# A layer with three kinds of heads on one core: small fp32 products become float32r with their parts stacked in the rows, and the scheduler gets other durations for narrow products

## The chip, the cores and the metric

One Trainium2 chip, one of its eight cores. The kernel is one program; its engines work side by side, each through its own list of instructions in order: TensorE (PE in the profile; PEld is its weight load), VectorE (DVE), ScalarE (ACT), GpSimd (POOL), and SyncE (SP), which here issues the large transfers. The metric is device microseconds of one execution: the median of a few runs. Beside it stands one execution that the profiler recorded.

## The reference

One decoder layer for 512 positions of width 1024, in fp32. Cut to what matters here:

```python
h = rmsnorm(x, norm1_w)
aq, ak, av, bq, bk, bv, br, ba, cq, ck, cv = split(h @ w_in)
# A (6 heads, dilated windows) and C (6 heads, blocks): softmax(q k^T / 8 + bias[bucket(distance)]) v
# B (4 heads, gated linear attention):
log_a = log_sigmoid(ba @ w_a2 + b_a) / 16          # ba: (512, 16), w_a2: (16, 128)
S_t = diag(exp(log_a_t)) S_{t-1} + k_t^T v_t ;  o_t = q_t S_t
y_b = rmsnorm_per_head(o) * gla_norm_w * silu(br)
x = x + concat(y_a, y_b, y_c) @ w_out
x = x + relu(rmsnorm(x) @ w_ff1)^2 @ w_ff2          # 1024 -> 4096 -> 1024
out = rmsnorm(x) * final_norm_w
```

The bias depends on the distance alone, so the kernel makes a table of 12 heads by 640 distances once; where a distance is masked, the table holds a huge number.

## The kernel before

**Numbers.** The large products are made of float32r halves: `hi` is the value rounded by an ACT copy to float32r, `lo` is the rest, made by a DVE subtraction; a product is `hi*hi + lo*hi + hi*lo`, three matmuls into one PSUM bank. The small products were left in plain fp32: the bias table (`vt`: `rb`, 34 rows, times `oneh`), the gate (`zps`: `wa2`, 16 rows, times `alT`), the row scale (`rps`: `ones` times `diag`, which spreads 1/rms of every position over all partitions), the attention transposes (`ptp`), the products of the gated heads (`lp`, `dps`, `ktp`, `op`, `up`) and probabilities times values (`po`).

**Stages on PE.** `first`: columns of the gated heads and of v (`av`, `bq`, `bk`). `v_proj(0)` (`vps`: 4 row tiles t, 24 matmuls each), `qk_proj` for the head pairs p = 0 to 2 (`qkps`: a q and a k bank per pair, 24 matmuls each), `v_proj(1)`, the pairs 3 to 5, `out_proj` (`ops`), then the feed-forward: 32 column tiles (`f`) in four chunks, each chunk followed by seven products of a Strassen-like scheme (`f2X`, `f2Y`, `f2Z`, `f2W`). Between these stand, in the same list, the gated heads (`gla`, `levels`, `carry`) and the attention (`attention`, `softmax`, `turned`, `values`).

**What sets the order.** All stages are Python generators; each yields an instruction, a list of them, a wait for an event, or a take of a resource (a PSUM bank of the groups mm, s, pt, o, g; a buffer; a weight pair `w`). `Plan.run` keeps a clock for every engine, adds `Op.cost` for every instruction, and always issues the candidate that could start first, ties by `prio` and age. Nothing of this runs on the chip: it fixes, at build time, the order in every engine's list. A wrong cost doesn't change what is computed, only where an instruction stands. `late` makes ACT the preferred engine in places where either may copy (`Any`).

**The gated heads' chain.** `gla` scales 16 columns (`alr`), turns them (`alps`), copies them to `alT`, multiplies by `wa2` (`zps`), and makes `la` and its running sum `b` on ACT and DVE. `levels` makes, for 7 levels of a halving scheme, `e` (differences of `b`), its exponential on ACT, and `kq` (DVE). Two levels at a time go to PE as 32 products `lp` of 32 rows and 64 columns; `lp` needs all four banks of s and pt, and DVE frees them with the masked copies `attn<-lmask,lp` (four a level). `v_out` empties each `vps` bank: a scaled copy `v`, then `sg` and `rg` (inputs of the output gate), then the bank is given back.

**Lines.** Every instruction is issued from one line of the planner, so the profile shows L117 for nearly all; the tile names tell them apart. In the changed kernel the same line is L123.

Of the kernel before, what the change touches and what calls it, by code (L numbers as in the profile page):

```python
# [22 lines left out]
BIG = 1e30  # L23
# [9 lines left out]
class Op:  # L33


    def __init__(self, eng, method, args, kw):
# [13 lines left out]
        if eng == "tensor":  # L50
            f = 4 if inner[-1].dtype == F32 and method == "matmul" else 1
            f = f / 2 if args[0].shape[0] == 64 else f / 4 if inner[-1].shape[0] == 32 else f
# [131 lines left out]
def hybrid_block_kernel(ctx: ExitStack, tc: tile.TileContext, xT_d, x_d, w0_d, wv_d, wqk_d, wo_d, w1_d, w2_d,  # L184
# [44 lines left out]
    lmask = consts.tile([128, len(LEVELS), 64], I32)  # L229
    rb = consts.tile([128, 128], F32)  # L230
    bav = consts.tile([128, 1], F32)
    wa2 = consts.tile([128, 128], F32)
    gw = consts.tile([128, 256], F32)
    ones = consts.tile([128, 128], F32)
    eps = consts.tile([128, 1], F32)
    rstd = consts.tile([128, NT], F32)
    nrstd = consts.tile([128, NT], F32)

    oneh = [slot("oneh", shape=(128, 320)) for _ in range(2)]
    alT = slot("alT", shape=(128, 512))  # L240
    xT = [slot("xT") for _ in range(KT)]
# [158 lines left out]
    def load_small():  # L400
        yield ("wait", ("xh", 1))
        for t, d in ((cst, cst_d), (rb[:34, :12], rb_d), (bav, ba_d), (wa2[:16], wa2_d)):
            yield POOL.dma_start(t, d)
        for i in range(2):
            yield POOL.dma_start(oneh[i][:34], oh_d[:, i * 320:(i + 1) * 320])
        fire("consts")
        spawn(bias_table(oneh), 1)
        yield POOL.dma_start(lmask, lm_d)
        for i in range(3):
            for e in range(2):  # L410
                yield POOL.memset(f32(klz[i][e][64 - 64 * e:128 - 64 * e]), 0.0)
        yield POOL.dma_start(gw, bass.AP(tensor=gw_d.tensor, offset=gw_d.offset, ap=[[0, 128], [1, 256]]))

    def row_scale():
# [3 lines left out]
        rsp = bank("mm", "rsp")  # L418
        yield [PE.matmul(rsp[:, 2 * t:2 * t + 2], ssx[:, t * 128:(t + 1) * 128], ones[:, :2], start=True, stop=True)
               for t in range(NT)]  # L420
# [8 lines left out]
        fire("rstd")  # L429
        diag = slot("diag")  # L430
# [11 lines left out]
        fire("R")  # L442

    def bias_table(oneh):
        yield ("wait", "first")
        for i in range(2):
            yield ("take", "mm")
            vt = bank("mm", "vt")
            yield PE.matmul(vt[:, :320], rb, oneh[i], start=True, stop=True)
            vals = slot("vals", shape=(12, 320))  # L450
            yield DVE.tensor_copy(vals, vt[:12, :320])
            give("mm")
            yield POOL.dma_start(tab[:, i * 320:(i + 1) * 320], vals)
        fire("tab")
# [39 lines left out]
    def gla():  # L494
# [4 lines left out]
        yield ("wait", "consts")  # L499
        alr = small("alr", (128, NT, 16))  # L500
# [6 lines left out]
        alps = bank("g", "alps")  # L507
        yield [PE.transpose(alps[:16, t * 128:(t + 1) * 128], alr[:, t, :], ident) for t in range(NT)]
# [126 lines left out]
    def carry(b, kB, qB):  # L635
# [17 lines left out]
        dg = small("dg", (128, 16))  # L653
        yield DVE.tensor_copy(dg, dps[:, :16])
        give("mm")
# [9 lines left out]
    def attention(e):  # L665
# [3 lines left out]
        for p in range(6):  # L669
# [14 lines left out]
            if ("sps", p) in plan.done:  # L684
                give("big")
                give("big")
                if p == 5:
                    for _ in range(3):
                        give("big")
                        give("w")  # L690
                    fire("scores")
# [75 lines left out]
    def v_out(g, t, acc):  # L767

        v = vS[g, t] = slot("v", shape=(128, 384))
        yield Any(ACT.activation(v, acc[:, :384], AF.Copy, scale=rstd[:, t:t + 1]),  # L770
                  DVE.tensor_scalar(v, acc[:, :384], rstd[:, t:t + 1], None, op0=OP.mult), late=dict(vector=late["copy"]))
        fire(("v", g, t))
        cs = slice(g * 128, g * 128 + 128)
        sg, rg = (x[:, t % 2, cs] for x in gates[t // 2])
        yield DVE.tensor_scalar(sg, acc[:, 384:], nrstd[:, t:t + 1], 80.0, op0=OP.mult, op1=OP.min)
        yield DVE.scalar_tensor_tensor(rg, acc[:, 384:], nrstd[:, t:t + 1], gw[:, cs], op0=OP.mult, op1=OP.mult)
        give("mm")
        if g and t % 2:
            spawn(gate(t // 2), 2)

    def v_proj(g):
# [6 lines left out]
        for t in range(NT):  # L788
# [10 lines left out]
            if t == 0:  # L799
                yield ("wait", "rstd")  # L800
                yield ("wait", "consts")
            spawn(v_out(g, t, acc), 1)

# [41 lines left out]
    def qk_proj(p):  # L845
        for i, out in enumerate((q_out, k_out)):
# [4 lines left out]
            give_w()  # L851
            spawn(out(p, acc), 1)

# [364 lines left out]
    def start():  # L1218
# [4 lines left out]
        plan.clock["scalar"] += 1.3  # L1223
        yield DVE.memset(ones, 1.0)
        yield DVE.memset(eps, EPS)
        for z in (rb, wa2, *oneh, alT):
            yield POOL.memset(z, 0.0)
        yield ("take", "mm")
        warm = bank("mm", "warm")
        for _ in range(WARM):  # L1230
            yield PE.matmul(warm[:, :128], ones, ones, start=True, stop=True)
        give("mm")
# [24 lines left out]
def _constants():  # L1257
    d = 511 - np.arange(640)
    oh = np.zeros((34, 640), np.float32)
    oh[_bucket(d), np.arange(640)] = -1.0  # L1260
    cnt = ((d >= 0) & (d <= 128)).astype(np.int32) + ((d >= 0) & (d % 4 == 0)) + ((d >= 0) & (d % 16 == 0))
    oh[32] = np.where(cnt > 0, -np.log(np.maximum(cnt, 1)), BIG)
    oh[33] = np.where(d >= 0, 0.0, BIG)
    ind = np.zeros((2, 12), np.float32)
    ind[0, :6] = 1.0
    ind[1, 6:] = 1.0
    cst = np.zeros((128, 1028), np.float32)
# [58 lines left out]
```

## Time and profile before

| | us |
|---|---|
| median of 3 runs | 596.07 (595.62 to 596.24) |
| the profiled execution's own time | 596.38 |
| its span, first to last instruction | 594.3 |
| PE busy | 581.6 (98%) |
| DVE busy | 428.2 (72%) |
| ACT busy | 321.4 (54%) |
| POOL busy | 18.2 (3%) |

How to read it: the span is that of one execution and lies 2.1 us under its time. A matmul's busy time holds its way through the array, so several overlap and a busy PE need not be at its peak; the distance from one matmul's end to the next's is what it costs in a row, and the chain of waits (what released what, from the last instruction back) shows these distances. An fp32 matmul has two records in the trace, a float32r matmul one. "Idle before" is an engine's wait, with what ended it.

### The profile page before, as it was taken

How to read it: one execution, taken by the hardware profiler on the slowest of the kernel's cores; microseconds unless marked ns; L12 is line 12 of the kernel's file. 1: busy time of each engine (PE TensorE's matmuls, PEld its weight loads, DVE VectorE, ACT ScalarE, POOL GpSimd, SP SyncE). 2: the span in 40 equal slices, each digit the busy share in tenths (PEclk: the TensorE clock that was granted, in tenths of full speed). 3: DMA queues.
4: the chain of work that ended last, by engine and by line, in shares of the span. 5: the costliest groups of instructions: out<-in, count | busy, mean ns of one | idle time of the engine just before them, and what ended most of it. 6: DMA issues, size and time to landing. Idle time of an engine off the chain costs nothing.

```text
span 594.3 us, 8155 instructions
## 1 busy us (share of the span) xinstructions
PE 581.6 (98%) x3021; PEld 481.1 (81%) x3021; DVE 428.2 (72%) x831; ACT 321.4 (54%) x593; POOL 18.2 (3%) x33
## 2 busy tenths in 40 slices
PE   9999999999999999999999999999999999999994
PEld 8977788878886778899888888888888888888883
DVE  5878976864798763565669964499935699764995
ACT  6643337766587663564466425475244664364544
POOL 6010000000000000000000000000000000000021
PEclk9999999999999999999999999999999999999998
DMA  8820431231423620093103642014631036201003
GB/s 299 338 74 2 142 96 47 80 99 57 140 74 113 221 71 2 1 364 139 64 0 117 239 142 71 1 56 157 215 104 35 2 121 235 69 0 36 1 0 142
DMA packets 20391, 61.91 MB, mean 104 GB/s; under 512 B 2544, under 2 KB 2586, under 8 KB 20352
## 3 DMA queue, kind: packets, MB, share of 16 engines
q1 hardware_dynamic: 19728, 60.37, 29.6%
q0 software_dynamic: 480, 1.02, 0.6%
q8 instruction: 24, 0.39, 0.3%
q14 instruction: 15, 0.12, 0.1%
q10 hardware_dynamic: 144, 0.01, 0.0%
HBM read 59.25 MB, written 2.13 MB: 103 GB/s over the span
## 4 chain that ended last, share of the span: by engine, by line
PE 89%; DVE 8%; ACT 1%; issue 1%; DVEq 0%
PE f L117 30%; PE f2X L117 12%; PE qkps L117 11%; PE ops L117 7%; PE f2Z L117 5%; PE vps L117 5%; PE f2Y L117 4%; PE sps L117 2%; PE po L117 2%; PE ptp L117 2%; PE av L117 2%; DVE x L117 1%; PE bq L117 1%; PE bk L117 1%; DVE attn L117 1%; PE f2W L117 1%
## 5 line engine op out<-in xcount | busy, mean ns | idle before, releaser
L117 PE MATMUL f<-yh,wh 128*128 128x512 f32 (+1 forms) x288 | 105.4, 366 | 0.0
L117 PE MATMUL f<-yl,wh 128*128 128x512 f32 (+1 forms) x288 | 105.3, 365 | 0.0
L117 PE MATMUL f<-yh,wl 128*128 128x512 f32 (+1 forms) x288 | 105.2, 365 | 0.0
L117 DVE TENSOR_TENSOR wl<-wraw,wh 128x1024 fp32r<-128x1024 f32 (+1 forms) x68 | 77.9, 1158 | 34.1 <-ACT wh L117 34.0
L117 ACT ACTIVATE wh<-wraw 128x1024 fp32r<-128x1024 f32 (+1 forms) x67 | 66.4, 1009 | 52.8 <-PE f L117 31.4
L117 DVE TENSOR_TENSOR wl<-w2raw,wh 128x1024 fp32r<-128x1024 f32 x48 | 59.1, 1241 | 47.2 <-ACT wh L117 43.6
L117 ACT ACTIVATE wh<-w2raw 128x1024 fp32r<-128x1024 f32 x48 | 50.3, 1052 | 53.4 <-PE f L117 36.8
L117 PEld LDWEIGHTS f<-yh,wl 128*128 128x128 f32 x288 | 54.3, 189 | 8.8
L117 PEld LDWEIGHTS f<-yl,wh 128*128 128x128 f32 x288 | 54.3, 189 | 8.7
L117 PEld LDWEIGHTS f<-yh,wh 128*128 128x128 f32 x288 | 54.3, 189 | 8.7
L117 PE MATMUL f2X<-wh,Ah 128*128 128x512 f32 x112 | 43.6, 389 | 0.0
L117 PE MATMUL f2X<-wh,Al 128*128 128x512 f32 x112 | 43.6, 389 | 0.0
L117 PE MATMUL f2X<-wl,Ah 128*128 128x512 f32 x112 | 43.6, 389 | 0.0
L117 PE MATMUL qkps<-xh,wh 128*128 128x512 f32 x96 | 40.3, 419 | 0.1
L117 PE MATMUL qkps<-xl,wh 128*128 128x512 f32 x96 | 37.6, 392 | 0.0
L117 PE MATMUL qkps<-xh,wl 128*128 128x512 f32 x96 | 37.6, 391 | 0.0
L117 ACT ACTIVATE P<-P,mn 128x512 f32<-128x512 f32 (+3 forms) x48 | 26.6, 554 | 11.5 <-DVE mn L117 11.3
L117 ACT ACTIVATE h<-f 128x512 f32<-128x512 f32 x32 | 18.7, 583 | 20.8 <-PE f L117 20.8
L117 DVE CUSTOM_DVE_ANT_0 P<-sps,nb 128x512 f32<-128x512 f32 (+3 forms) x48 | 22.3, 480 | 8.8 <-PE sps L117 8.5
L117 PE MATMUL vps<-wh,xh 128*128 128x512 f32 x64 | 27.9, 437 | 0.0
L117 ACT ACTIVATE junk<-x 128x512 f32<-128x512 f32 x16 | 10.1, 630 | 30.4 <-DVE x L117 30.4
L117 ACT ACTIVATE Ah<-s 128x512 fp32r<-128x512 f32 x32 | 18.8, 619 | 13.9 <-DVE s L117 13.9
(223 smaller groups left out, 1210.6 us busy)
## 6 DMA issues: line engine op xcount, KB each, us to landing
wraw<-in_w SPq DMA_DIRECT2D x32, 512.0 KB, 3.4
w2raw<-in_w SPq DMA_DIRECT2D x32, 512.0 KB, 4.1
wraw<-in_wqk SPq DMA_DIRECT2D x12, 512.0 KB, 3.5
wraw<-in_wv SPq DMA_DIRECT2D x8, 512.0 KB, 6.6
wraw<-in_wo SPq DMA_DIRECT2D x8, 512.0 KB, 3.7
nb<-tab SPq DMA_DIRECT2D x12, 256.0 KB, 3.9
wraw<-in_w SPq DMA_DIRECT2D x8, 264.0 KB, 6.8
xT<-in_xT SPq DMA_DIRECT2D x8, 256.0 KB, 6.7
```

The lines of the kernel that those rows point to most:

```text
L117: getattr(getattr(self.nc, op.eng), op.method)(*op.args, **op.kw)
```

## The change

**Numbers.** `rb`, `oneh`, `wa2`, `alT`, `ones` and `diag` become float32r, with the parts of both factors stacked in the rows, so that one matmul sums the parts' products: rows 0 to 31 of `rb` hold the table's rounded values and rows 32 to 63 the rest, against the same one-hot rows twice; the three rows for masks stand at 64. `wa2` holds hi, hi and lo at rows 0, 32 and 64, `alT` holds hi, lo and hi there (the 16 columns are scaled into three groups of 32 and turned together). The row scale alone becomes two matmuls, with `dh` and `dl`. A new stream, `stacked`, rounds the small tables (3 ACT copies, 2 DVE subtractions); `bias_table` and the gate wait for it. `alT` is now copied by ACT, and one DVE subtraction follows.

**Scheduler.** Other costs for PE, two lines of them:

```diff
-            self.cost = 0.002 + (max(n, 250) / 2400 * f if method == "matmul" else 0.054)
+                self.cost = 0.0135 + long
```

(`long` is max(n, 250)/2400; a transpose counts 0.109, an fp32 matmul of 32 rows 0.031, other fp32 matmuls at least 0.212.)

**Moves.** `v_out` copies `v` on ACT always, copies the gate's columns to `rg` on ACT, gives the bank back, and makes `sg` and `rg` on DVE from SBUF with a later priority; `dg` is copied by ACT; of the weight pairs given back after the last attention, two come after pair 4 instead; `v_out`, `q_out` and `k_out` get priority 0.5.

```diff
 def load_small():
-        for t, d in ((cst, cst_d), (rb[:34, :12], rb_d), (bav, ba_d), (wa2[:16], wa2_d)):
+        for t, d in ((cst, cst_d), (rbx[:32], rb_d[:32]), (rb[64:67, :12], rb_d[32:]), (bav, ba_d), (wax[:16], wa2_d)):
...
+        spawn(stacked(), 1)
 def row_scale():
+        yield ACT.activation(dh, diag, AF.Copy)
+        yield DVE.tensor_tensor(dl, diag, f32(dh), op=OP.subtract)
...
-        yield PE.matmul(rps, ones, diag, start=True, stop=True)
+        yield [PE.matmul(rps, ones, d, start=(d is dh), stop=(d is dl)) for d in (dh, dl)]
+    def stacked():
+        yield ACT.activation(rb[:32, :12], rbx[:32], AF.Copy)
+        yield DVE.tensor_tensor(rb[32:64, :12], rbx[:32], f32(rb[:32, :12]), op=OP.subtract)
+        yield ACT.activation(wa2[:16], wax[:16], AF.Copy)
+        yield ACT.activation(wa2[32:48], wax[:16], AF.Copy)
+        yield DVE.tensor_tensor(wa2[64:80], wax[:16], f32(wa2[:16]), op=OP.subtract)
+        fire("stacked")
 def bias_table(oneh):
+        yield ("wait", "stacked")
 def gla():
-            yield DVE.tensor_scalar(alr[:, t, :], acc_v[t][:, 256:272], rstd[:, t:t + 1], None, op0=OP.mult)
+            yield DVE.tensor_scalar(alr[:, t, :, :16], acc_v[t][:, None, 256:272].to_broadcast([128, 3, 16]), rstd[:, t:t + 1],
+                                    None, op0=OP.mult)
...
-        yield DVE.tensor_copy(alT[:16], alps[:16, :])
+        yield ACT.activation(alT[:96], alps[:96], AF.Copy)
+        yield DVE.tensor_tensor(alT[32:64], alps[32:64], f32(alT[32:64]), op=OP.subtract)
         give("g")
+        yield ("wait", "stacked")
 def carry(b, kB, qB):
-        yield DVE.tensor_copy(dg, dps[:, :16])
+        yield ACT.activation(dg, dps[:, :16], AF.Copy)
 def v_out(g, t, acc):
-        yield Any(ACT.activation(v, acc[:, :384], AF.Copy, scale=rstd[:, t:t + 1]),
-                  DVE.tensor_scalar(v, acc[:, :384], rstd[:, t:t + 1], None, op0=OP.mult), late=dict(vector=late["copy"]))
+        yield ACT.activation(v, acc[:, :384], AF.Copy, scale=rstd[:, t:t + 1])
...
-        yield DVE.tensor_scalar(sg, acc[:, 384:], nrstd[:, t:t + 1], 80.0, op0=OP.mult, op1=OP.min)
-        yield DVE.scalar_tensor_tensor(rg, acc[:, 384:], nrstd[:, t:t + 1], gw[:, cs], op0=OP.mult, op1=OP.mult)
+        yield ACT.activation(rg, acc[:, 384:], AF.Copy, scale=nrstd[:, t:t + 1])
         give("mm")
+        yield ("prio", 2)
+        yield DVE.tensor_scalar(sg, rg, 80.0, None, op0=OP.min)
+        yield DVE.tensor_tensor(rg, rg, gw[:, cs], op=OP.mult)
```

The rest of the diff moves the zeroing of these tiles (POOL zeroes `alr` too) and lays out the constants on the host in the new rows.

**What the lists become.** On PE the matmuls stay the same but for one more in `rps`. From the first `f` on, PE's list differs only in where the last `yps` transposes stand; DVE's and ACT's there differ by instructions that change places with a neighbour or two.

First place: DVE from the end of `first` to the gate's `la` (`alr` the 16 gate columns, `vals` the bias table's values, `Rn` the row scale, `wl` a weight's lo half). Before:

```order
L117 TENSOR_SCALAR alr<-av_118,rstd 128x16
L117 COPY vals<-vt 12x320
L117 TENSOR_TENSOR wl<-wraw,wh 128x1024
L117 TENSOR_SCALAR Rn_95<-rps 128x512
L117 COPY alT<-alps 16x512
L117 COPY vals<-vt 12x320
L117 TENSOR_SCALAR la<-zps,bav 128x512
```

Now:

```order
L123 TENSOR_SCALAR alr<-av_121,rstd 128x3x16
L123 COPY vals<-vt 12x320
L123 TENSOR_TENSOR wl<-wraw,wh 128x1024
L123 TENSOR_SCALAR Rn_98<-rps 128x512
L123 COPY vals<-vt 12x320
L123 TENSOR_TENSOR alT<-alps,alT 32x512
L123 TENSOR_SCALAR la<-zps,bav 128x512
```

The copy of `alT` has left DVE, and a subtraction that makes its lo rows stands behind the second `vals`.

Second place: DVE between the first and the second group of `lp` (a level is told by its shape: 4x64 and 8x32 are the first group's, 16x16 and 32x8 the second's). Before:

```order
L117 TENSOR_SCALAR sg<-vps,nrstd 128x128
L117 SCALAR_TENSOR_TENSOR rg<-vps,nrstd,gw 128x128
L117 TENSOR_TENSOR qk<-qB,kB 128x512
L117 TENSOR_TENSOR kq<-kB,e 128x16x16
L117 TENSOR_TENSOR kq<-qB,e 128x16x16
L117 TENSOR_TENSOR e<-b 128x32x8 x2
L117 COPY_PREDICATED attn_540<-lmask,lp 128x4x64
L117 TENSOR_TENSOR kq<-kB,e 128x32x8
L117 TENSOR_TENSOR kq<-qB,e 128x32x8
L117 TENSOR_TENSOR e<-b 128x64x4 x2
L117 COPY_PREDICATED attn_541<-lmask,lp 128x4x64
```

Now:

```order
L123 TENSOR_TENSOR qk<-qB,kB 128x512
L123 TENSOR_TENSOR kq<-kB,e 128x16x16
L123 TENSOR_TENSOR kq<-qB,e 128x16x16
L123 TENSOR_TENSOR e<-b 128x32x8 x2
L123 COPY_PREDICATED attn_572<-lmask,lp 128x4x64
L123 COPY_PREDICATED attn_573<-lmask,lp 128x4x64
L123 COPY_PREDICATED attn_574<-lmask,lp 128x4x64
L123 TENSOR_TENSOR kq<-kB,e 128x32x8
L123 TENSOR_TENSOR kq<-qB,e 128x32x8
L123 TENSOR_TENSOR e<-b 128x64x4 x2
L123 COPY_PREDICATED attn_575<-lmask,lp 128x4x64
```

`sg` and `rg` have left this stretch, and three of the masked copies that free a bank stand together ahead of the next level's `kq`.

Third place: PE from the first group of `lp` to the first weights of the next stage (`dps` and `ktp` are small products of `carry`). Before:

```order
L117 MATMUL lp<-kq 128x64 x32
L117 MATMUL dps<-cst,qk 128x4 x4
...
L117 MATMUL lp<-kq 128x64 x32
L117 MATMUL ktp<-cst,ek 128x128 x3
```

Now:

```order
L123 MATMUL lp<-kq 128x64 x32
...
L123 MATMUL dps<-cst,qk 128x4 x4
...
L123 MATMUL ktp<-cst,ek 128x128 x3
...
L123 MATMUL lp<-kq 128x64 x32
```

Left out are `vps` matmuls. Between `first` and the first group of `lp` they are 51 before and 60 now; between the first and the second group 21 before and 27 now; between the second and the third 18 before, and now 9 with 15 `qkps`; ahead of the last group 6 with 9 `qkps` before, and 18 `qkps` now. Up to the first `op` (a product of the gated heads) all 96 `vps` are done in both lists; of `qkps` there are 21 before and 54 now.

## Rows read from the trace of the kernel before

**Rows 1.** The page's chain that ended last, shares of the span by engine

```profile
PE 89%; DVE 8%; ACT 1%; issue 1%; DVEq 0%
```

**Rows 2.** Chain in order of time (start us, us, what): feed-forward and end

```profile
346.05 43.52 PE f L117 x192
...
558.21 4.77 PE f2Y L117 x21
...
579.85 0.61 DVE x L117
```

**Rows 3.** The same chain, from the end of first to the gate

```profile
30.23 0.54 PE vt L117 x2
...
31.46 1.00 PE rps L117 x2
...
33.16 0.44 PE alps L117 x4
...
33.92 0.78 PE vt L117 x2
...
35.39 0.87 PE zps L117 x2
```

**Rows 4.** The same chain, gated heads

```profile
55.73 1.96 PE lp L117 x58
57.70 0.81 PE ktp L117 x3
58.50 5.40 PE vps L117 x18
63.90 1.98 PE lp L117 x64
...
70.25 1.07 PE lp L117 x26
...
74.72 0.84 PE op L117 x8
```

**Rows 5.** Timeline of PE (start us, us, instructions, [idle before]), 53 to 70 us

```profile
53.45 0.39 PE L117 MATMUL vps<-wl,xh 128*128 128x512 f32 x1
54.07 1.06 PE L117 MATMUL lp<-kq 32*128 32x64 f32 x6 [0.23 <-DVE attn L117]
55.73 1.96 PE L117 MATMUL lp<-kq 32*128 32x64 f32 x58 [0.60 <-DVE dg L117]
...
69.40 0.44 PE L117 MATMUL lp<-kq 32*128 32x64 f32 x6
```

**Rows 6.** Windows: A:B us, PE, PEld, DVE, ACT, POOL busy, PEclk, DMA, GB/s

```profile
57.70:61.10 3.40, 3.40 (x10) 2.81 (x11) 3.40 (x11) 2.50 (x4) 0.00 (x0) 0.50 0.00 0
61.10:74.70 13.60, 13.20 (x139) 10.71 (x139) 12.81 (x23) 3.83 (x5) 0.00 (x0) 1.00 0.47 155
...
257.00:563.00 306.00, 306.00 (x1445) 257.52 (x1444) 219.25 (x308) 153.21 (x234) 0.00 (x0) 1.00 0.29 101
563.00:580.00 17.00, 16.97 (x75) 13.71 (x73) 16.99 (x29) 7.99 (x16) 5.27 (x4) 1.00 0.00 0
```

**Rows 7.** Timeline of DVE, 52 to 54 us: one level of the gated heads

```profile
52.49 0.42 DVE L117 TENSOR_TENSOR kq<-qB,e 128x256 f32<-128x256 f32 x1
52.82 0.75 DVE L117 TENSOR_TENSOR e<-b 128x256 f32<-128x256 f32 x2
53.49 1.09 DVE L117 COPY_PREDICATED attn<-lmask,lp 128x256 f32<-128x256 int32 x3
54.49 0.42 DVE L117 TENSOR_TENSOR kq<-kB,e 128x256 f32<-128x256 f32 x1
```

**Rows 8.** Timeline of ACT: a weight's hi half in first, the row scale's copy

```profile
18.54 0.63 ACT L117 ACTIVATE wh<-wraw 128x528 fp32r<-128x528 f32 x1
...
32.50 0.60 ACT L117 ACTIVATE R<-rps 128x512 f32<-128x512 f32 x1 [1.24 <-PE rps L117]
```

**Rows 9.** What PE waited for: us in total, times, longest us

```profile
PE sps L117 <- DVE mn L117: 0.5, 1, 0.5
```

More of the change, by code (lines that the diff above doesn't have):

```diff
@@ L50, in __init__ @@
         if eng == "tensor":
-            f = 4 if inner[-1].dtype == F32 and method == "matmul" else 1
-            f = f / 2 if args[0].shape[0] == 64 else f / 4 if inner[-1].shape[0] == 32 else f
-            self.cost = 0.002 + (max(n, 250) / 2400 * f if method == "matmul" else 0.054)
+            wide, long = inner[-1].dtype == F32, max(n, 250) / 2400
+            if method != "matmul":
+                self.cost = 0.109
+            elif wide and inner[-1].shape[0] == 32:
+                self.cost = 0.031
+            elif wide:
+                self.cost = 0.002 + max(n / 600 / (1 + (args[0].shape[0] == 64)), 0.21)
+            else:
+                self.cost = 0.0135 + long
         elif eng == "scalar":
@@ L237, in hybrid_block_kernel @@
     nrstd = consts.tile([128, NT], F32)
-    oneh = [slot("oneh", shape=(128, 320)) for _ in range(2)]
-    alT = slot("alT", shape=(128, 512))
+    oneh = [slot("oneh", F32R, (128, 320)) for _ in range(2)]
+    alT = slot("alT", F32R)
+    alr = slot("alr", shape=(128, NT, 3, 32))
     xT = [slot("xT") for _ in range(KT)]
@@ L418, in row_scale @@
         rsp = bank("mm", "rsp")
-        yield [PE.matmul(rsp[:, 2 * t:2 * t + 2], ssx[:, t * 128:(t + 1) * 128], ones[:, :2], start=True, stop=True)
+        yield [PE.matmul(rsp[:, 2 * t:2 * t + 2], ssx[:, t * 128:(t + 1) * 128], f32(ones[:, :2]), start=True, stop=True)
                for t in range(NT)]
@@ L507, in gla @@
         alps = bank("g", "alps")
-        yield [PE.transpose(alps[:16, t * 128:(t + 1) * 128], alr[:, t, :], ident) for t in range(NT)]
-        yield DVE.tensor_copy(alT[:16], alps[:16, :])
+        yield [PE.transpose(alps[:96, t * 128:(t + 1) * 128], alr[:, t].rearrange("p a b -> p (a b)"), ident) for t in range(NT)]
+        yield ACT.activation(alT[:96], alps[:96], AF.Copy)
+        yield DVE.tensor_tensor(alT[32:64], alps[32:64], f32(alT[32:64]), op=OP.subtract)
         give("g")
+        yield ("wait", "stacked")
         yield ("take", "o")
@@ L686, in attention @@
                 give("big")
+                if p == 4:
+                    give("w")
+                    give("w")
                 if p == 5:
@@ L851, in qk_proj @@
             give_w()
-            spawn(out(p, acc), 1)
+            spawn(out(p, acc), 0.5)
     gates = []
@@ L1223, in start @@
         plan.clock["scalar"] += 1.3
-        yield DVE.memset(ones, 1.0)
+        yield DVE.memset(f32(ones), 1.0)
         yield DVE.memset(eps, EPS)
-        for z in (rb, wa2, *oneh, alT):
+        for z in (f32(rb), f32(wa2), f32(oneh[0]), f32(oneh[1]), alr, f32(alT)):
             yield POOL.memset(z, 0.0)
@@ L1230, in start @@
         for _ in range(WARM):
-            yield PE.matmul(warm[:, :128], ones, ones, start=True, stop=True)
+            yield PE.matmul(warm[:, :128], f32(ones), f32(ones), start=True, stop=True)
         give("mm")
@@ L1258, in _constants @@
     d = 511 - np.arange(640)
-    oh = np.zeros((34, 640), np.float32)
-    oh[_bucket(d), np.arange(640)] = -1.0
+    oh = np.zeros((67, 640), np.float32)
+    for i in (0, 32):
+        oh[i + _bucket(d), np.arange(640)] = -1.0
     cnt = ((d >= 0) & (d <= 128)).astype(np.int32) + ((d >= 0) & (d % 4 == 0)) + ((d >= 0) & (d % 16 == 0))
[L1262 to L1266, printed above, removed]
+    few = np.where(cnt > 0, -np.log(np.maximum(cnt, 1)), BIG).astype(np.float32)
+    oh[64] = (few.view(np.int32) & ~4095).view(np.float32)
+    oh[65] = np.where(cnt > 0, few - oh[64], 0.0)
+    oh[66] = np.where(d >= 0, 0.0, BIG)
+    ind = np.zeros((3, 12), np.float32)
+    ind[:2, :6] = 1.0
+    ind[2, 6:] = 1.0
     cst = np.zeros((128, 1028), np.float32)
```

17 lines of the change are left out of this document (9 added, 8 removed).

## The prediction

> **What bounds the kernel now.** I read the chain that ended last first: 89% of it is PE [rows 1]. That alone could mean a busy or a waiting PE, so I looked at distances. In the feed-forward 192 matmuls of 512 columns follow each other in 43.52 us [rows 2], 0.227 us each; from 257 to 563 us PE is busy for all 306 us of the window, at a granted clock of 1.00 (2.4 GHz) [rows 6]. So the second half runs at one matmul after the other, and nothing in it can be gained but by removing matmuls. What can change lies ahead of it. There the chain shows fp32 products dearer than their columns [rows 3], two groups of small products at which PE waited [rows 4, 5], and a stretch of 3.4 us at a granted clock of 0.50 (1.2 GHz) [rows 6]. PE is the engine to follow; each of the others matters only where PE waits for it.
>
> Does time gained early arrive at the end? The tail from 563 us is DVE's: it is busy for 16.99 of 17.00 us there [rows 6], but the chain enters it from PE's `f2Y`, which ends at 562.98, and its last add into x starts at 579.85 [rows 2]. Between 257 and 563 us DVE has 87 us idle (306 less 219.25 [rows 6]), so its tail isn't held up by earlier work and starts when PE gets there. I take early gains as passed on whole.
>
> **Part by part. The fp32 products.** A float32r matmul of 512 columns costs 0.227. `zps` takes 0.87 as fp32 and becomes one matmul: 0.64 less. `rps` takes 1.00 and becomes two: 0.55 less. The two `vt` took 0.54 each without their wait [rows 3]; 320 columns of float32r lie between 0.14 (by columns) and 0.227, and I take 0.15, since the columns scale: 0.78 less for both (0.63 at worst). `alps` keeps its four transposes (0.44 [rows 3]); more rows come out, the columns that go in are the same. Sum: **1.97 us** off PE.
>
> **What it adds elsewhere.** `stacked` puts three small ACT copies and two small DVE subtractions into `first`. ACT makes the last weight's hi half of `first` at 18.54 [rows 8] and PE ends `first` only at 30.23 [rows 3]; even at the price of a full 512-wide copy (0.60 [rows 8]) three copies are 1.8 us, against some 8 us of lead that ACT has by then. The price is nothing as long as that lead stands, 1.8 us if it were gone. POOL's queue gets one transfer and one zeroing more ahead of the others; its tables are first needed shortly before `vt` at 30.23, and PE waits for no transfer there before. `dh` and `dl` (one copy of 0.60, one subtraction of 0.61 as the add of [rows 2]) lie behind the six `vps` that now stand ahead of `rps`. The output gate's columns cost ACT eight more copies, at most 0.60 each, and DVE as many instructions as before; ACT is the idler engine.
>
> **The wait before the second `vt`.** PE idled 0.33 and the product took 0.78 for 0.54 [rows 3]: 0.57 lost. It takes the bank that `rps` gives back after a copy on ACT and one on DVE, about 1.3 us behind `rps`. Now six `vps` (1.36) and `alps` (0.44) lie between: covered, **0.57 us** off.
>
> **The gate's chain, followed once.** From 30.23: `vt` 0.15, six `vps` 1.36, `rps` 0.45, six `vps` 1.36, `alps` 0.44, that is 33.99; `vt` 0.15 and six `vps` bring PE to `zps` at 35.50. Its input is ready 0.60 (ACT) and 0.61 (DVE, behind the second `vals`) after `alps`: 35.2 to 35.4. The new subtraction fits by 0.1 to 0.3 us; if it doesn't, PE waits and all of the gate's chain with it, a few tenths. `zps` ends at 35.73 where it ended at 36.26, and 42 `vps` (9.52) later PE is at the first `lp` at 45.25. Before, PE reached it at 45.7 with 9 `vps` less behind it.
>
> **The second group of `lp`.** The `vps` that started at 53.45 was through at 53.68; a group takes 1.98 [rows 4]; it ended at 57.69 [rows 4, 5]. Waits for the masked copies cost 57.69 - 53.68 - 1.98 = 2.03 us. Now: the first group ends at about 47.3, and 27 `vps` (6.12), `dps` (0.9) and `ktp` (0.33) bring PE to the second at 54.6 (a transpose is 0.11 by `alps`, and `dps` has eight records of that size). On DVE one of a level's two `kq` costs 0.33 (52.49 to 52.82), its `e` pair 0.67, three masked copies 1.00 [rows 7]. In the new list stand, between the second level's `kq` (done at 45.3 to 46.0) and the last masked copy of the first group: three `e` pairs ahead of the copies and one among them, three `kq` pairs, eight copies (2.7) and two 512-wide products (1.2), together 8.6: 53.9 to 54.6. PE arrives at that time or just after. **2.0 us** off, at worst 1.2.
>
> **The clock.** At 57.70, after 4.0 us in which PE had nothing but `lp` and waits, the granted clock fell to 0.50 until 61.10 [rows 6]. `ktp` took 0.81 for 0.33 and 18 `vps` 5.40 for 4.08 [rows 4]: 1.80 lost. The third group of `lp`, 1.98 us long with full matmuls on both sides, brought no fall: 1.00 from 61.1 to 74.7 [rows 6]. In the new order every group stands so. I take **1.8 us** off. The Trainium skill, "TensorE: Matmul & The Clock Gate", section "Why this matters for your kernels", warns of idle gaps between bursts of matmuls several times longer than the 0.23 and 0.60 here. By that rule the fall would not come from these waits and would not leave with them, and the sum would be 1.8 us smaller; the fall in this trace speaks against the rule as it stands.
>
> **The last group.** Half a group is 0.99; its first records started at 69.40 [rows 5] and it ended at 71.32 [rows 4], so 0.9 was lost to masked copies. Now 18 `qkps` (4.08) lie between the third group and it: 0.7 off. The waits around `dps` (0.3) go too, since it now stands behind three more `vps`.
>
> **Sum by the first `op`:** 1.97 + 0.57 + 2.0 + 1.8 + 0.7 + 0.3 = 7.3 us. A count confirms it without any of these terms. From 30.23 on, the new list holds up to the first `op`: 96 `vps` and 54 `qkps` (150 x 0.227 = 34.0), `rps`, `zps`, `vt`, `alps` (1.4), three and a half groups of `lp` (some 7.5 with their first matmul), `dps`, `ktp`, `up` (1.7): 44.6, so `op` at 74.9. Before it came at 74.72 [rows 4] with 33 `qkps` less done: 33 x 0.227 - 0.2 = 7.3.
>
> **The attention.** Its order is new throughout, and the trace of before can't show its waits. It had one wait of 0.5 at `sps` [rows 9]; some such waits go, some come. Bounds: 1.0 off (that one and as much again in smaller ones) to 2.0 on (one more like the second `lp`). Following DVE through the first pair I find PE waiting some tenths at `sps`, no more, and I take 0.5 off, nearest to the row. **The feed-forward's** neighbours change places by one weight subtraction (1.1 us) at most, with its inputs ready one product (5.44) ahead: nothing, at worst 0.5, since PE had no wait in those 306 us while DVE had 87 idle.
>
> **The forecast.** 7.3 + 0.5 = 7.8 off the profiled execution's 596.38 is 588.6. The median of the runs is 0.3 under that execution: **588.3**, with 586.0 to 589.4 as its own range.
>
> **Rivals.** (1) The clock falls all the same: small products cause it, not the waits. For it: `lp` and `dps` stand close again, with few `vps` between; against it: the third group kept 1.00 around it [rows 6], and no wait is left that I can find. 590.1. (2) The scheduler's order brings new waits at the attention, two of the size of the second `lp`: 592.3. The stretch from 257 us on has no slack that could give them back. (3) The new order gives nothing: what is gained at `lp` is lost at `sps`, and only the passes are left. 596.1 - 2.0 = 594.1, hardly beyond what can be told from no change (about 0.2%, 1.2 us). (4) Slower: the attention of a pair now starts while the gated heads still hold DVE, and PE waits for softmax at every one of the six pairs. At 2.0 us each that is 12.2, less the 0.5 above: 588.3 + 12.2 = 600.5; it decides from 1.5 us a pair on, where 9 us are lost. For it: the earlier start, and ACT's extra copies. Against it: 0.5 us was the longest such wait in all six pairs, and `qkps` or `vps` stand between the steps as before.
>
> **How the numbers follow.** Forecast 0.58, better than its range 0.03, (1) 0.15, (2) 0.11, (3) 0.08, (4) 0.05. Range: from 586.0, the attention's and the feed-forward's waits all gone and small ones with them, to 593.0, case (2) with its bounds; (3) and (4) are left out. Faster: all but (4), half of (3) and a little of (2): 0.88; same 0.07; slower 0.05.
>
> **What would show it.** Right: `zps` a single record of some 0.23 us in the chain; the first `op` near 74.9 with no wait over 0.3 at any `lp`; PEclk at 1.00 from 57 to 62 us; `f` starting some 7.8 earlier; the stretch from there to the end as long as before. Wrong: a window at 0.50 in the gated heads or the attention; PE waiting for `mn`, `th` or a masked copy by more than 1 us in sum; a longer tail.

## The result and the profile after

The changed kernel takes **592.89 us** (median of 6 runs, 592.38 to 593.49); the runs of the kernel before that stood beside it have a median of 596.15. The ratio is 0.9932, with a 95% interval of 0.9913 to 0.9951. So it is faster by 3.3 us, inside the range by 0.1 us, but by less than half of the 7.8 us that the sum promised. The profiled execution took 592.38 us with a span of 590.6, 3.7 less than before.

First the chain that ended last, as the page gives it for the changed kernel, by engine; it answers to [rows 1]:

```profile
PE 83%; DVE 12%; ACT 2%; issue 1%
```

PE's share fell from 89 to 83%, and DVE's rose from 8 to 12%: the path now leaves PE more often. Where it does is seen in the chain in order of time (start us, us, what), here from the end of `first` to the first softmax step, then two rows of the second half. It answers to [rows 2 to 4]:

```profile
29.14 0.15 PE vt L123
...
30.68 0.47 PE rps L123 x2
...
32.97 0.15 PE vt L123
...
34.49 0.44 PE zps L123
...
44.49 1.94 PE lp L123 x64
46.44 0.89 PE vps L123 x3
...
54.03 1.94 PE lp L123 x64
...
61.64 1.98 PE lp L123 x64
63.62 2.30 DVE attn L123 x6
...
80.15 0.68 DVE P L123
80.85 0.04 issue
80.89 1.23 PE sps L123 x4
...
341.13 43.52 PE f L123 x192
```

Up to 63.6 us the chain stays on PE, and no wait stands at any `lp`. One short wait hides inside a row: `zps` takes 0.44 us where 0.23 were expected. A matmul's weights are loaded ahead of it by PEld (for the `vps` before `zps` at 33.88, the matmul itself starting at 34.10), and the load for `zps` waited for DVE's subtraction into `alT`:

```profile
34.43 0.19 PEld L123 LDWEIGHTS zps<-alT,wa 128*128 128x128 f32 x1 [0.37 <-DVE alT L123]
```

Where this load doesn't wait (e3, e7 and e13 below), `zps` takes 0.23. From 63.6 us on, for 17 us, the chain runs through DVE (masked copies, weight subtractions, the q and k of the first pairs, small steps of the gated heads) until `sps` waits for it at 80.89, by 0.37 us. PE isn't idle up to there, it works on `qkps`. The feed-forward is the same to the hundredth of a microsecond, 43.52 us for 192 matmuls, and starts 4.92 us earlier than in [rows 2].

The windows of the changed kernel (A:B us, then busy time of PE, PEld, DVE, ACT and POOL, PEclk, DMA share, GB/s) that answer to [rows 6]:

```profile
57.70:61.10 3.40, 3.40 (x17) 2.82 (x16) 3.37 (x11) 1.79 (x3) 0.00 (x0) 1.00 0.60 179
61.10:74.70 13.60, 13.60 (x142) 11.12 (x141) 11.56 (x20) 3.27 (x4) 0.00 (x0) 1.00 0.23 78
```

The window at 0.50 is gone and PE is busy throughout. What PE waited for (us in total, times, longest) answers to [rows 5, 9]:

```profile
PE sps L123 <- DVE mn L123: 1.2, 3, 0.6
...
PE f2Z L123 <- DVE x L123: 0.9, 1, 0.9
PE yps L123 <- DVE yl L123: 0.6, 1, 0.6
PE ptp L123 <- ACT th L123: 0.3, 1, 0.3
```

The waits at `lp` have left the list. Before, they were these:

```profile
PE lp L117 <- DVE attn L117: 0.6, 2, 0.4
...
PE lp L117 <- DVE dg L117: 0.6, 1, 0.6
```

In their place stand waits at softmax, 1.2 at `sps` where it was 0.5, and a new one at `yps`.

**Where the gain went.** Three points of the two traces can be laid side by side. At the first `vt` the changed kernel is 1.09 us ahead (29.14 to 30.23): this can't be put down to the change, since five of the traces below whose lists are the same up to there (the changed kernel, e4, e6, e11, e12) have that `vt` at 29.1 to 30.1. At the first `op`, at 74.70 where it was 74.72, it has done 33 more `qkps`, 7.5 us of work; less the 1.09 that makes **6.4 us** won between 30 and 75 us. At the first `f` the lead is 4.92, less 1.09: **3.8 us**. So 2.6 us were given back between 75 and 252 us. The list of waits shows about half of it: from there on the waits at `sps`, `ptp` and `yps` come to 2.3 us, and to 1.0 before. After that the list costs 0.3 us more up to PE's end (the longer wait of `f2Z` for x), and the end behind PE 9.0 us where it was 8.0.

### The profile page after: what moved, and what is told of

Read it like the earlier page. It is cut to its first block, busy times and chain, and to the rows that moved or that the text cites. A ratio compares the mean times of both kernels' runs of the same rounds, so it can differ in the third digit from the quotient of the medians.

```text
span 590.6 us, 8146 instructions
## 1 busy us (share of the span) xinstructions
PE 577.4 (98%) x3018; PEld 476.0 (81%) x3018; DVE 426.2 (72%) x830; ACT 327.2 (55%) x610; POOL 18.6 (3%) x35
## 4 chain that ended last, share of the span: by engine, by line
PE 83%; DVE 12%; ACT 2%; issue 1%
PE f L123 30%; PE f2X L123 11%; PE ops L123 7%; PE vps L123 7%; PE qkps L123 6%; PE f2Z L123 6%; PE f2Y L123 3%; DVE wl L123 2%; PE po L123 2%; PE ptp L123 2%; PE av L123 2%; PE sps L123 2%; DVE x L123 2%; DVE P L123 1%; DVE Al L123 1%
## 5 line engine op out<-in xcount | busy, mean ns | idle before, releaser
L123 PE MATMUL ops<-wh,mh 128*128 128x512 f32 x64 | 26.0, 407 | 0.0
L123 PE MATMUL f2Z<-wh,Ah 128*128 128x512 f32 x64 | 25.0, 390 | 0.9 <-DVE x L123 0.9
```

The lines of the kernel that those rows point to most:

```text
L123: getattr(getattr(self.nc, op.eng), op.method)(*op.args, **op.kw)
```

## The experiments

The change has three parts that can be made apart: the **products** in float32r with stacked parts, the **moves** (copies of the output gate and `dg` to ACT, an earlier `give`, priorities of 0.5), and the scheduler's new **durations** for PE. The first four runs take them apart, later ones split the durations by time and by kind. The time from the first `vt` to the first `f` is read from each profile, and leaves out the start and the feed-forward. Ratios are to the runs of the kernel before on the same chip.

| kernel | products | moves | durations | median us | ratio, 95% interval | `vt` to `f` us |
|---|---|---|---|---|---|---|
| before | fp32 | no | old | 596.1 to 596.5 | | 226.6 |
| e2_new_costs | fp32 | no | new | 595.86 | 0.9986 [0.9973, 0.9999] | 225.8 |
| e3_f32r_only | float32r | no | old | 600.74 | 1.0068 [1.0043, 1.0094] | 231.0 |
| e5_moves_only | fp32 | yes | old | 598.17 | 1.0025 [1.0005, 1.0046] | 229.1 |
| e1_old_costs | float32r | yes | old | 592.63 | 0.9926 [0.9899, 0.9952] | 225.0 |
| e14_no_f32r | fp32 | yes | new | 594.10 | 0.9952 [0.9934, 0.9970] | 224.2 |
| e10_v_out_before | float32r | all but the gate's | new | 593.57 | 0.9954 [0.9937, 0.9972] | none |
| changed kernel | float32r | yes | new | 592.89 | 0.9932 [0.9913, 0.9951] | 222.8 |
| e4_lp62 | float32r | yes | new, `lp` 0.062 | 592.66 | 0.9930 [0.9912, 0.9948] | 224.0 |
| e7_old_then_new | float32r | yes | old to 72 us, then new | 596.23 | 0.9987 [0.9964, 1.0009] | 225.1 |
| e6_new_then_old | float32r | yes | new to 72 us, then old | 588.53 | 0.9858 [0.9821, 0.9896] | 219.5 |
| e11_late_dense_old | float32r | yes | from 72 us: dense old | 590.73 | 0.9895 [0.9875, 0.9915] | 221.7 |
| e12_late_rest_old | float32r | yes | from 72 us: all else old | 592.12 | 0.9920 [0.9902, 0.9937] | 222.7 |
| e13_dense_old | float32r | yes | new, dense old | 590.84 | 0.9901 [0.9883, 0.9919] | 222.0 |

**Old durations under the rest of the change (e1).** Its edit:

```diff
-            wide, long = inner[-1].dtype == F32, max(n, 250) / 2400
-            if method != "matmul":
-                self.cost = 0.109
...
-                self.cost = 0.0135 + long
+            f = 4 if inner[-1].dtype == F32 and method == "matmul" else 1
+            f = f / 2 if args[0].shape[0] == 64 else f / 4 if inner[-1].shape[0] == 32 else f
+            self.cost = 0.002 + (max(n, 250) / 2400 * f if method == "matmul" else 0.054)
```

> The changed kernel with the scheduler's durations for PE of before; the float32r products and all moves stay. Theory A (the new durations gain some 4.7 us up to the first `op`, the passes only 1.7, and 2.6 is given back later at softmax, by the new order): 18 `vps` stand between the first two `lp` groups, as few as before (21), so PE waits 1.5 to 2.5 us at the second group and a window at a granted clock of 0.50 follows it; by the first `op` the lead on the kernel before is 2 to 3 us, and it ends at 593 to 595. Rival B (the order brought nothing, the passes all of it): as the changed kernel, 592.5 to 593.5, with no wait at `lp`. Rival C (the copies moved to ACT cause the waits at softmax): waits at `sps` and `ptp` in the attention stay near 4 us.

Measured: 592.63, the same as the changed kernel. It lies 0.4 us below theory A's range, and in rival B's. But it isn't rival B: the waits at `lp` are there. The rows are PE's timeline (with the idle time before each; two more waits of 0.17 stand between these), then a window, as above:

```profile
66.77 0.40 PE L117 MATMUL lp<-kq 32*128 32x64 f32 x2 [0.62 <-DVE attn L117]
...
68.47 1.89 PE L117 MATMUL lp<-kq 32*128 32x64 f32 x26 [0.17 <-DVE attn L117]
```

```profile
68.52:75.35 6.83, 6.83 (x38) 5.66 (x39) 3.29 (x6) 0.00 (x0) 0.00 (x0) 0.50 0.00 0
```

They stand at the last group, not at the second, and in this run a fall of the granted clock to 0.50 over 6.83 us followed, which costs half of it. Not every run has it: three of its six runs have a mean granted clock of 0.997 to 0.998 and take 590.5 to 591.5, three have 0.990 to 0.992 and take 593.8 to 594.7. That is 3 us, as 6.83 us at half speed make it (3.4). In its runs at 0.997 or more this kernel beats the changed one by 2 us: its list loses at `lp`, and from the first `op` to the first `f` it takes 1.6 us less than the kernel before for the same work (178.49 us with 258 `qkps`, against 182.12 with 267). Rival C falls with it: the copies on ACT are in it, and PE has no wait at `sps`.

**Durations alone (e2)** is the same edit the other way round, made in the kernel before.

> The kernel before with the scheduler's new durations for PE alone; no product is float32r and nothing is moved to ACT. 30 `vps` and `dps` stand between the first two `lp` groups. Theory A: no wait over 0.3 us at `lp`, granted clock 1.00 all the way from 10 to 580 us, lead at the first `op` 4 to 5 us, then 1 to 3 given back at `sps` and `ptp`: 592.5 to 594.5. Rival B: the lead at the first `op` is under 1 and the time 595.5 to 596.5. Rival C: the waits in the attention stay as short as before (2.4 us over the pure products), and the time is 591.5.

Measured: 595.86, no better than rival B's bound, though the granted clock was 1.00 all the way. The first part of A holds (no long wait at `lp`), but a wait came up that A hadn't in it, at a `vps` for DVE's `rg`:

```profile
PE vps L123 <- DVE rg L123: 1.4, 1, 1.4
```

So the lead at the first `op` is 2.3 us and not 4 to 5 (42 `qkps` done where it was 21, 2.5 us later from the first `vt`), and 1.4 of it are given back up to the first `f`, within A's 1 to 3.

**float32r alone (e3)** leaves durations, `v_out`, `dg`, the gives and the priorities as before.

> The kernel before with the products in float32r and the stacked parts alone; durations, priorities and the output gate's copies as before. Theory A: 18 `vps` and `dps` between the first two `lp` groups, PE waits 2 us or more at the second, the granted clock falls to 0.50 after it; gain 1.7 (passes) and 0.6 (second `vt`), 593.5 to 595. Rival B: the whole gain of the changed kernel, 592.5 to 593.5. Rival D (the clock's fall in the run of before was chance): the wait is there, but the granted clock stays at 1.00, and it ends 1.8 earlier than A says, 592 to 593.

Measured: 600.74, 4.5 us *slower* than before; no theory had that. The timeline of DVE, and the row of PE that waited for it:

```profile
53.97 0.35 DVE L117 TENSOR_SCALAR sg<-vps,nrstd 128x128 f32<-128x128 f32 x1 [0.48 <-ACT v L117]
...
54.57 0.42 DVE L117 TENSOR_TENSOR kq<-qB,e 128x256 f32<-128x256 f32 x1
54.91 0.34 DVE L117 SCALAR_TENSOR_TENSOR rg<-vps,nrstd,gw 128x128 f32<-128x128 f32 x1
...
55.40 0.47 PE L117 MATMUL vps<-wh,xh 128*128 128x512 f32 x1 [4.37 <-DVE rg L117]
```

`vps` needs a bank, and `v_out` gives one back only after `rg`, which stands in DVE's list behind products and masked copies of the gated heads. PE stood still for 4.37 us, as the first of these windows shows; the others are two falls of the granted clock behind it:

```profile
51.00:55.40 4.40, 0.03 (x2) 0.04 (x1) 3.92 (x13) 2.18 (x4) 0.00 (x0) 1.00 0.00 0
55.75:59.17 3.42, 3.42 (x30) 2.49 (x32) 1.37 (x3) 0.00 (x0) 0.00 (x0) 0.50 0.09 19
72.82:79.65 6.83, 6.83 (x35) 5.57 (x32) 3.80 (x7) 0.00 (x0) 0.00 (x0) 0.50 0.00 0
```

The two falls take 5.1 us of work, the wait 4.4, against some 2 won by the passes; the kernel before has a fall of its own (1.8 us of work) and its waits at `lp` (2.0). Set against each other these make 3.7 us, where 4.5 were measured.

**The moves alone (e5).** The kernel before with, among others:

```diff
-        yield DVE.tensor_copy(dg, dps[:, :16])
+        yield ACT.activation(dg, dps[:, :16], AF.Copy)
...
-        yield DVE.tensor_scalar(sg, acc[:, 384:], nrstd[:, t:t + 1], 80.0, op0=OP.mult, op1=OP.min)
+        yield ACT.activation(rg, acc[:, 384:], AF.Copy, scale=nrstd[:, t:t + 1])
         give("mm")
```

> The kernel before with the moves alone (the output gate's copies and `dg` on ACT, the earlier `give`, the priorities of 0.5); products in fp32, durations of before. Theory A, mended: the moves only take away a wait that the kernel before doesn't have, so the waits at `lp` (2 us at the second group) and the window at 0.50 stay: 595 to 596.5. Rival E (the moves carry most of the gain by themselves): the gated heads are 2 to 4 us shorter and it ends at 592 to 594.

Measured: 598.17, slower than both theories. Here it is the other move that PE waits for. The timeline of ACT, PE's row, and two windows:

```profile
51.50 0.63 ACT L117 ACTIVATE e<-e 128x512 f32<-128x512 f32 x1 [1.50 <-DVE e L117]
52.04 0.17 ACT L117 ACTIVATE dg<-dps 128x16 f32<-128x16 f32 x1
...
52.26 0.90 PE L117 MATMUL ktp<-cst,ek 128*128 128x128 f32 x3 [2.36 <-ACT dg L117]
```

```profile
50.99:57.82 6.83, 5.56 (x15) 4.50 (x16) 5.16 (x16) 1.82 (x4) 0.00 (x0) 0.50 0.00 0
74.89:78.30 3.41, 3.41 (x10) 2.66 (x9) 2.83 (x6) 0.00 (x0) 0.00 (x0) 0.50 0.00 0
```

`dg` frees the bank of `dps`, and stands in ACT's list behind an `e` that itself waits for DVE. In the changed kernel it stands ahead of that `e` (48.15 and 48.23 us in its trace) and nobody waits. The wait is about as long as what the kernel before loses at `lp` (2.0 us by the prediction's working); what makes this kernel slower goes with the clock: nine of its ten runs have a mean granted clock of 0.988 to 0.990 and take 597.4 to 599.3 us, the tenth has 0.994 and takes 595.82. So neither the products nor the moves gain anything alone; what a part is worth depends on the list that it stands in.

**The gate's step of before in the changed kernel (e10).** The step `v_out` alone is put back; the bank of `vps` is again freed by DVE after `rg`.

> The changed kernel, with the output gate's step written as before: the bank of a `vps` product is given back by DVE after `rg`, not by ACT. Theory A, mended by the first four runs (in them PE waited 4.4 us for `rg` where only the products were float32r, 1.4 where only the durations were new, and not at all in the kernels with the moved copies): the bank comes back behind the masked copies on DVE, PE waits 1 to 4 us at `vps` between the first two `lp` groups, and it ends at 594 to 597. Rival: the new order alone keeps PE fed, no wait for `rg` over 0.3 us, 592 to 593.

Measured: 593.57, 0.7 us above the changed kernel, between the two. Its profiled execution took 2057.62 us and can't be laid beside the others, so whether PE waits for `rg` here, and where the 0.7 us lie, stays open.

**The changed kernel without float32r (e14).** The kernel before with the moves of e5 and the durations of e2.

> The changed kernel without its float32r products: the moves and the new durations, with the six products in fp32 as before. By the sum of the passes (1.7 us) and the wait behind the second `vt` (0.6) it takes 2.3 us more than the changed kernel, 595.2. Rival J (what the products gain or lose is the list that they bring about: 21 `vps` between the first two `lp` groups, where PE waits again, up to 2 us and with a fall of the clock): 596 to 598.

Measured: 594.10. The products in float32r (`vt`, `zps`, `rps`) are worth 1.2 us in the final list, about half of what the sum of the passes said (2.3 with the second `vt`). The traces show why: by the first `op` this kernel is 2.4 us behind the changed one, as the sum had it (its lead on the kernel before is 4.0 there, with 36 `qkps` done), and from there to the first `f` it gives back 1.5 us where the changed kernel gives back 2.6. Rival J's waits did not come.

**`lp` with its measured duration (e4).** The edit is one number, 0.062 for 0.031.

> The changed kernel with 0.062 us for each of the narrow `lp` products in the scheduler instead of 0.031 (a group of 32 takes 1.94 to 1.98 us in the trace, which is 0.062 each). Theory A: up to the first `op` the list is the same but for three `vps` or `qkps`, so the lead there is the same within 0.3 us; the attention of the first pairs is mixed otherwise, with the third `up` and its `op` later, and what is given back there changes by up to 1.5 us either way: 591.5 to 594. A rival (the wrong duration of `lp` is what makes the waits at softmax): the waits of the attention fall from 4.2 to 2.4 us and it ends at 591.

Measured: 592.66, as A says; the number itself doesn't make the waits. A's lead at the first `op` did not come in the profiled run: it was 4.2 us, not 6.4, with a fall of the clock ahead of it. PE's timeline, and two windows:

```profile
44.38 2.01 PE L123 MATMUL lp<-kq 32*128 32x64 f32 x64
46.60 1.03 PE L123 MATMUL dps<-cst,qk 128*128 128x4 f32 x8 [0.21 <-PE lp L123]
...
48.58 0.84 PE L123 MATMUL ktp<-cst,ek 128*128 128x128 f32 x3 [0.15 <-ACT dg L123]
```

```profile
43.80:48.69 4.89, 4.53 (x79) 3.56 (x78) 4.89 (x14) 1.66 (x4) 0.00 (x0) 1.00 0.00 0
48.69:52.11 3.42, 3.42 (x10) 2.85 (x11) 3.42 (x12) 1.12 (x2) 0.00 (x0) 0.50 0.02 5
```

Three `vps` less stand between `lp`, `dps` and `ktp` than in the changed kernel; PE waited 0.36 us in 4.89, and the clock fell. In the changed kernel the same products, with those three `vps` more and no wait, kept 1.00. In e13 (below) `lp`, `dps`, three `vps` and `ktp` stand as close as here and without a wait, and kept 1.00 too. In e1 and e7 the same two waits stand at the same place (0.21 + 0.16 and 0.25 + 0.16 us), and no fall came there.

**New durations early or late (e6, e7).** Both kernels keep both formulas and choose by the scheduler's own clock. The line of e6 (e7 has `<` for `>=`):

```diff
-        self.clock[op.eng] = end = t + op.cost
+        cost = op.old if op.eng == "tensor" and t >= 72.0 else op.cost
+        self.clock[op.eng] = end = t + cost
```

> The changed kernel, whose scheduler goes by the new durations for PE up to 72 us of its own clock (about the first `op`) and by those of before after that. The list is the changed kernel's up to the first softmax step; the third `up` comes later still. Theory F (the new durations make the waits of the attention): excess at `sps`, `ptp` and `yps` falls from 4.2 + 0.8 to that of before, 590 to 591. Rival G (the waits come from the third `up` and its `op`, which now stand behind the first softmax steps so that DVE has both at once): the waits for `mn` and `th` stay at 1.5 us or more, 592 to 593.5.

> The other way round: durations of before up to 72 us of the scheduler's clock, the new ones after that. Up to the first softmax step the list is that of the changed kernel with the old durations (592.6, of which 590.5 to 591.5 in its runs with a granted clock of 0.997 and 593.8 to 594.7 at 0.990 to 0.992); all three `up` stand ahead of the first softmax step. Theory F: the waits at `sps`, `ptp` and `yps` come back, 1.5 to 2.5 us longer than that: 594 to 595, or 592.5 to 593.5 in runs at 0.997. Rival G: only `yps` (0.6) and `f2Z` (0.3) wait longer, and it stays within 1 us of it.

Measured: 588.53 and 596.23. This is the clearest answer of the study, and it is theory F's, though e6 goes beyond it and e7 is 1 to 2 us above it (594.5 to 595.0 in its runs at 0.997, where 592.5 to 593.5 was expected). Early, the new durations gain 4.1 us (592.63 to 588.53) or 3.3 (596.23 to 592.89); late, they lose 4.4 (588.53 to 592.89) or 3.6 (592.63 to 596.23). The two effects hardly depend on each other. A part of the early gain is the clock: taking e1's and e7's runs at 0.997 or more alone (medians 591.0 and 594.8), the early gain is 2.5 or 1.9 us, and the late loss 4.4 or 3.7. Rival G falls: in e6 the third `up` starts at 92.3 us, later than in the changed kernel (88.5), and it costs nothing; in e7 all three stand ahead of the first `sps`, and the waits come.

e6 also comes out as the prediction had forecast the changed kernel. From the first `op` to the first `f` it takes 173.95 us with 234 `qkps`, 0.7 less than the kernel before needs for the same work (182.12 less 33 x 0.227 = 174.6); the changed kernel, with the same work, takes 177.22, 2.6 more.

How the late list loses is seen in the two chains, from the second pair's softmax on. The changed kernel:

```profile
101.01 0.47 PE sps L123 x2
101.50 0.04 DVE P L123
...
107.77 0.19 DVE P L123
107.98 0.04 issue
108.02 0.44 PE sps L123 x2
...
114.38 0.49 ACT th L123
114.87 0.04 issue
114.91 1.09 PE ptp L123 x8
```

and e6:

```profile
101.14 0.50 PE sps L126 x2
101.65 0.69 PE qkps L126 x3
102.34 0.46 PE sps L126 x4
102.80 0.69 PE qkps L126 x3
...
104.41 0.22 PE ptp L126 x2
```

In the changed kernel the path goes over to DVE for 6.5 us and to ACT after it; it does so again from 150.4 to 167.9, at 177.3 and at `yps` (231.0 to 233.4). In e6 three or more `qkps`, `vps` or `ops` stand between nearly any two softmax steps and the path stays on PE from 101 us to the end of `ops`, with waits of hundredths.

**Which duration (e11, e12, e13).** As e6, but from 72 us on only the float32r products go back to the old duration (0.215 us for one of 512 columns; e11), or only all others (e12); e13 has the old one for them from the start. The line of e13:

```diff
-                self.cost = 0.0135 + long
+                self.cost = 0.002 + long
```

> The changed kernel; from 72 us of the scheduler's clock on, the 512-wide float32r products alone are counted with the duration of before (0.215 instead of 0.227 us each). Theory H (this one number makes the waits of the attention: a shorter duration lets the scheduler put more `qkps` between two softmax steps, and these are what PE works on while DVE has `mn`): as the kernel with all durations of before from there, 588 to 589.5, excess over the pure products from 75 to 252 us about 8 us. Rival I (the transposes or the fp32 products): 592 to 593.5, excess 11 us or more.

> The counterpart: from 72 us on the transposes and the fp32 products are counted as before, the 512-wide float32r products as in the changed kernel. Theory H: 592 to 593.5, excess from 75 to 252 us 11 us or more. Rival I: 588 to 589.5.

> The changed kernel with the old duration of the 512-wide float32r products from the start; all other durations are the new ones. Theory H: the attention's list is much like that of the one before, 24 `vps` between the first two `lp` groups as in the changed kernel; `rps` now stands right behind the first `vt`, where PE may wait some tenths: 588.3 to 590. Rival I: 592 or more.

Measured: 590.73, 592.12 and 590.84: e12 as H says, e11 and e13 between H and I. The float32r products' number brings back 2.2 us of the 4.4, all others 0.8; together they make more than the sum. In e11's profile PE has only one short wait for `mn`, but two new ones:

```profile
PE qkps L127 <- DVE tq L127: 0.6, 1, 0.6
...
PE ops L127 <- DVE tk L127: 0.5, 1, 0.5
PE sps L127 <- DVE mn L127: 0.4, 1, 0.4
```

So H is half right: the waits of the second pair go with that number, while the list of the last pairs is one more draw. That the scheduler overfills with 0.215 and underfills with the true 0.227 (0.227 us each by the 43.52 of 192) was read from the lists, where with the one three `qkps` stand between nearly any two `sps` pairs, and with the other two pairs often follow each other at once; a rule that would foretell the last pairs wasn't found.

## Why the prediction was right or wrong

**The sum by the first `op`, 7.3 us: right in kind, 0.9 too large.** Measured 6.4. All signs that it named came true: no wait at any `lp`, granted clock 1.00 from 57 to 62 us, the first `op` at 74.70 (forecast 74.9, from a start 1.09 earlier). The passes came out at 1.74 us for 1.97 (`vt` 0.15 twice, `rps` 0.47, `zps` 0.44 in the chain above). What is missing is a wait: the prediction let the new subtraction into `alT` fit "by 0.1 to 0.3 us", and it didn't fit, since the load of `zps`'s weights wants `alT` before the matmul does, and DVE ended it 1.4 us after `alps` where 1.2 was counted. The larger part of the 0.9 is the first matmul behind each `lp` group, which takes 0.2 us more: three `vps` behind `lp` take 0.89, elsewhere 0.68 to 0.70. The sum had one price for a matmul wherever it stands, and the count that confirmed it had 7.5 us for the groups with their first matmuls, which took some 8.0. Leaving the products in fp32 (e14) costs 2.4 us by the first `op`, as the sum said, of which 1.2 are left at the end.

**The clock, 1.8 us: the fall left, as forecast; its cause is shown in part, its size isn't.** In five of the profiled kernels, that of before among them, the clock fell in the gated heads, each time with waits of PE ahead: from 0.33 us (e5's second fall) and 0.36 (e4) to 4.4 (e3). No profiled kernel without such waits had a fall, and e13, with the narrow products as close together as in e4, kept 1.00; so rival (1), small products alone as a cause, isn't supported. But waits alone don't suffice either: in e7 1.1 us of them, at the place where they brought a fall in e1, brought none in the profiled run, nor did 1.4 us in e2, and what decides it stays open. That the fall would leave with the waits was right for this kernel, whose runs differ by 1.1 us in all. The Trainium skill, "TensorE: Matmul & The Clock Gate", section "Why this matters for your kernels", holds idle gaps between bursts responsible that are longer than any wait here but the one of 4.37 us; by that rule only e3 would have had a fall, and four other traces show one. How much the fall in the trace of before had cost is not settled, since its kernel was never run without the waits alone, but its other runs speak against 1.8 us. Of the runs beside the experiments, four have a mean granted clock of 0.998, too high for a fall of 3.4 us (which takes 0.003 off the mean), and take 595.5 to 595.7, 0.7 to 0.9 less than the profiled 596.38. None of the four was profiled.

**The attention, 0.5 off: the step that failed.** It cost 2.6 us. The prediction took 1.0 off to 2.0 on as bounds and chose a gain, "nearest to the row" of before; but the row belonged to another list. I followed DVE through the first pair only, found tenths there, and let that stand for six pairs: the losses lie in the second (`sps` at 108, `ptp` at 114.9) and behind 150 us. Rival (2), new waits at the attention, is what happened, with small waits (0.6 at most in the list) in place of two large ones; its 592.3 is 0.6 from the result. The result lies in the range only because the range reached up to this rival's bound, 593.0; the forecast's own range ended at 589.4. Its cause, by e6 and e7, is the new durations behind the first `op`, and not the moves or the third `up`. With the old ones there (e6) the attention is 0.7 us off, near the 0.5 that was forecast, and the time is 588.53 for a forecast of 588.3.

**Early gains passed on whole: half right.** From the first `f` on they are (4.92 us, and still 4.92 at the `f` of 341). In the attention it depends on the list: the changed kernel gave back 2.6 of the 6.4 us. That the chain runs through DVE from 63 to 81 us is not the reason, for in e6 it runs through DVE from 64 to 81 us too, with the same early lead, and nothing is given back.

**The tail, "as long as before": wrong by 1.3 us in the profiled run.** `f2Z` waits 0.9 to 1.0 where it waited 0.6, in all kernels with the new duration of the dense products late (0.6 in those with the old one). From the first `f` to PE's end these take 0.3 us more, from there to the last instruction 0.1 to 1.0 more, the most in the changed kernel; why it varies stays open.

**Rival (4)** did not come (its 12.2 isn't six times 2.0; nothing rests on it). Rival (3), that the passes alone are left, gave 594.1; the runs make the change 3.3 us faster, and the change without its float32r products (e14) takes 1.2 us more.

## What to carry to other kernels

Measure the parts of such a change in the company in which they will stand: here the products alone cost 4.5 us, the moves alone 2 (both with falls of the clock), and both together gained 3.6. Where a list scheduler sets the order, truer durations are no gain by themselves; split them by stage, look where the chain leaves the bounding engine, and keep cover between steps that wait for another engine's result. The best kernel of the study takes the new durations up to the first `op` and the old ones after: 588.53 us, ratio 0.9858 [0.9821, 0.9896]. Don't queue what frees a bank behind work that itself waits (4.37 us in e3, 2.36 in e5). Look at the loads (PEld) too: a wait for a matmul's weights can hide inside its row.

## What the runs showed of the hardware

- The granted clock's fall is a matter of the run: one kernel (e1) ran at 590.5 to 591.5 us with a mean of 0.997 to 0.998, and at 593.8 to 594.7 with 0.990 to 0.992. A single profile of such a kernel can mislead by 3 us. The kernel before shows the same: four runs at 0.998 take 595.5 to 595.7, twelve at 0.991 or 0.992 take 597.6 to 599.1.
- A fall came behind as little as 0.36 us of listed waits in 4.9 us of mostly narrow products (e4), and lasted 3.42 us there and 6.83 in e1. Waits of 0.37 and 0.41 us at the same place brought none in e1 and e7, and one of 1.4 us none in e2.
- The first float32r matmul of 512 columns behind a group of `lp` takes about 0.2 us longer than those that follow (three `vps` 0.89), behind `dps` 0.1 (three 0.80), and behind `ktp` no more (21 in 4.79).
- A wait of the weight load doesn't appear among PE's listed waits: `zps` took 0.44 us where its load waited for `alT`, and 0.23 in e3, e7 and e13, where it didn't.
- A group of 32 `lp` products is 64 records and takes 1.94 to 1.98 us, 0.062 each and not the 0.031 of the new duration; correcting it changed nothing that can be measured (592.66 to 592.89).
